# One step of gate and up columns, one block of sums: the down weights' sums spread over the steps, in tiles that they share with that step's product

## The chip, the cores and the metric

The kernel runs on one core of a Trainium2 chip. Five engines work side by side there, each in its own written order, and wait for one another through semaphores: TensorE (PE, matmuls into PSUM), VectorE (DVE, element by element), ScalarE (ACT, casts, copies and activations), GpSimd (POOL, hardly used in the part that matters here) and SyncE (SP), which issues the transfers between the chip's main memory and the on-chip tiles. The metric is device microseconds of one execution; lower is better. Before the change the median of 3 runs is 1890.63 us (1890.01 to 1895.91).

## The reference

One decoder layer over 1024 tokens of width 1024: three attention mixers, a merge and an output projection, then a gated MLP with a short convolution. The change lies in the MLP:

```python
def conv_ffn(h, w_gate, w_up, conv_w, conv_b, w_down):
    a = h @ w_gate
    a = lax.conv_general_dilated(a, conv_w[:, None, :], window_strides=(1,),
                                 padding=[(CONV_WIDTH - 1, 0)],
                                 dimension_numbers=('NWC', 'WIO', 'NWC'),
                                 feature_group_count=a.shape[-1]) + conv_b
    return (jax.nn.gelu(a) * (h @ w_up)) @ w_down
```

`h` is [1024, 1024], `w_gate` and `w_up` are [1024, 2816], `w_down` is [2816, 1024], all float32.

## The kernel before

The matrix products are made from pairs of rounded numbers: each operand is split into a high half (an ACT cast, `qhi`, L1544) and a low half (a DVE subtraction, `qlo`, L1545), and three matmuls (L1572, L1573, L1574) stand for one exact product. Large products are made by a scheme with seven block products instead of eight: operands are cut in four quarters, and sums of quarters are multiplied (`seven`). Its right operands (the activations, B11, T1 and so on) stay on chip; its left operands are the weights and sums of the weights (S1 to S4).

`gate_up` walks over the 2816 columns in 10 steps of two column blocks (f0 = 2, 4, ..., 20; the pair f0 = 0 is made earlier). A step loads two pieces of w_gate and two of w_up (`qraw`, L1556, three buffers), makes the sums (`qS`, L1563) and halves, and calls `seven` twice, once into `ga`, once into `ua`. The tiles `ua` have the names xh6 and xh7. Then DVE multiplies the activated gate `gc` by `ua` (L1641), and SP stores it to `s_act` (L1643). Inside `seven`, PE writes a partial product into a T tile of PSUM (two buffers), DVE adds u1 to it (`u2`, then after a second product on the same tile `u3`, L1589), ACT copies one quarter of the result straight to its destination (L1599), and DVE adds the other three.

The product with `w_down` (`down`) needs the sums S1 to S4 of its own weights. They are made ahead, during `gate_up`: `down_sums(k)` loads two blocks of 128 rows of w_down into the tiles xh4 and xh5 (L1654, L1655), makes four sums in place on DVE (L1660) and stores them to `s_sums` (L1661). There are 11 such blocks; the text calls them by k, 0 to 10. At the start of `down`, xh4 and xh5 take the first activation rows (L1683).

Outside of `down`'s transfers the order of the instructions on each engine is not that of the code: a scheduler places each as early as its own estimate of times lets it go, subject to the tiles. So the sums, written for the steps f0 = 8 to 18, stand earlier on DVE: one block after another, as soon as xh4 and xh5 are free again. Products of neighbouring calls of `seven` also overlap on PE.

Of the kernel before, what the change touches and what calls it, by code (L numbers as in the profile page):

```python
# [12 lines left out]
F32 = mybir.dt.float32  # L13
# [5 lines left out]
P = 128  # L19
D = 1024  # L20
T = 1024
# [146 lines left out]
class Builder:  # L168
# [1461 lines left out]
    def gate_up(self, sp):  # L1630

        nc, a = self.nc, self.a
        hs = [slice(0, 512), slice(512, 1024)]
        for f0 in range(2, NF, 2):
            ga = self.gate_tiles(sp)
            self.seven(self.left_ops(a["w_gate"], f0), [[z[:, 2 + s.start:2 + s.stop] for s in hs] for z in ga])
            gc = self.convolve(f0, ga, sp)
            ua = [self.t(self.xp, [P, T], F32, f"xh{6 + i}") for i in range(2)]
            self.seven(self.left_ops(a["w_up"], f0), [[z[:, s] for s in hs] for z in ua])
            for i in range(2):  # L1640
                nc.vector.tensor_tensor(out=gc[i], in0=gc[i], in1=ua[i], op=ALU.mult)  # L1641
                if f0 + 2 < NF:
                    nc.sync.dma_start(self.s_act[(f0 + i) * P:(f0 + i + 1) * P, :], gc[i])  # L1643
            if 8 <= f0 < 20:
                for k in range((f0 - 8) * 11 // 12, (f0 - 6) * 11 // 12):
                    self.down_sums(k)
        return gc

    def down_sums(self, k):

        nc, w = self.nc, self.a["w_down"]
        lo, hi = slice(0, 512), slice(512, 1024)
        top, bottom = (self.t(self.xp, [P, T], F32, f"xh{n}") for n in (4, 5))
        nc.sync.dma_start(top, w[k * P:(k + 1) * P, :])  # L1654
        nc.sync.dma_start(bottom, w[(k + NF // 2) * P:(k + NF // 2 + 1) * P, :])  # L1655
        for n, o, x, y, op in ((0, bottom[:, hi], top[:, hi], bottom[:, hi], ALU.add),
                               (2, top[:, hi], top[:, lo], top[:, hi], ALU.subtract),
                               (1, top[:, lo], bottom[:, hi], top[:, lo], ALU.subtract),
                               (3, bottom[:, lo], bottom[:, lo], top[:, lo], ALU.subtract)):
            nc.vector.tensor_tensor(out=o, in0=x, in1=y, op=op)  # L1660
            nc.sync.dma_start(self.s_sums[n, k], o)  # L1661
# [262 lines left out]
```

## Time and profile before

| | |
|---|---|
| median of 3 runs | 1890.63 us |
| lowest, highest | 1890.01, 1895.91 us |
| the profiled execution's own time | 1894.6 us |
| its span, first to last instruction | 1892.8 us |
| mean granted clock of TensorE | 0.996 |
| busy: PE, DVE, ACT, POOL | 98%, 71%, 49%, 21% |
| DMA, mean over the span | 121 GB/s |

The profile is of one execution, and its times count from the span's first instruction. PE writes and reads deeply pipelined, so consecutive matmuls of 0.39 us start 0.227 us apart. The steps of `gate_up` lie between about 1263 and 1685 us, the sums of the down weights (L1660) between 1298.3 and 1447 us, the first matmul of `down` (L1787) at 1668.5. A wait is booked on the engine that stands idle, with the instruction that ended it. For SP the profile shows when it issues a transfer, and the chain of waits shows for some transfers the time from issue to landing.

### The profile page before, as it was taken

The page shows a single profiled execution, that of the slowest core. Times are in us where ns is not written, and L with a number is a line of the kernel's source. Part 1 is how long each engine was busy: PE and PEld are TensorE (multiplying, and loading weights), DVE is VectorE, ACT ScalarE, POOL GpSimd, SP SyncE. Part 2 cuts the span into 40 slices and gives each one's busy share as a digit, 9 for nine tenths or more (in the row PEclk, how much of TensorE's full clock was granted, in tenths as well). Part 3 has the DMA queues.
Part 4 walks back from the last instruction along what each step waited for, and adds up shares of the span by engine and source line. Part 5 has one row for each costly group of instructions (what it writes and reads, how often), then busy time and mean ns, then how long its engine had stood idle before and what let it go on. Part 6 is the DMA issues. An engine that isn't in the chain of part 4 may idle for free.

```text
span 1892.8 us, 30670 instructions
## 1 busy us (share of the span) xinstructions
PE 1847.5 (98%) x10663; PEld 1623.0 (86%) x10663; DVE 1345.5 (71%) x2825; ACT 926.1 (49%) x1987; POOL 406.2 (21%) x586
## 2 busy tenths in 40 slices
PE   8999999999999999999989999999999999999999
PEld 8999999999988888888878888888877888878887
DVE  7664777776875766856588766679887677776865
ACT  4443566565544654555587423445333334344443
POOL 2223655565522323213132220000000000000000
PEclk9999999999999999999999999999999999999999
DMA  6345222323221132222343745525666322267433
GB/s 209 112 140 136 81 81 74 81 82 89 76 74 56 54 95 66 65 65 57 108 142 104 239 154 175 172 84 173 229 216 205 100 67 82 80 203 236 139 100 123
DMA packets 201472, 228.38 MB, mean 121 GB/s; under 512 B 43634, under 2 KB 149122, under 8 KB 201317
## 3 DMA queue, kind: packets, MB, share of 16 engines
q1 hardware_dynamic: 201252, 226.29, 38.9%
q8 instruction: 84, 1.38, 0.3%
q14 instruction: 72, 0.58, 0.1%
q0 software_dynamic: 64, 0.13, 0.0%
HBM read 162.12 MB, written 64.25 MB: 120 GB/s over the span
## 4 chain that ended last, share of the span: by engine, by line
PE 78%; DVE 10%; DMA 6%; issue 3%; ACT 2%; POOL 1%; SPq 0%; DVEq 0%; ACTq 0%; POOLq 0%
PE D L259 9%; PE D L258 9%; PE D L260 9%; PE T L797 4%; PE O L821 2%; PE S L685 2%; PE O L820 2%; PE S L259 2%; PE S L260 2%; PE S L258 2%; PE S L689 2%; PE S L1789 2%; PE S L1787 2%; PE S L1788 2%; PE S L1573 1%
## 5 line engine op out<-in xcount | busy, mean ns | idle before, releaser
L713 ACT ACTIVATE p<-S,mf 128x512 f32<-128x512 f32 (+3 forms) x320 | 174.2, 548 | 102.7 <-DVE mf L704 94.4
L805 DVE TENSOR_TENSOR pTl<-T,pTh 128x512 fp32r<-128x512 f32 (+2 forms) x248 | 151.0, 616 | 81.1 <-ACT pTh L804 79.4
L258 PE MATMUL D<-whi,xh 128*128 128x256 f32 (+2 forms) x680 | 199.8, 294 | 2.4 <-ACT whi L234 2.4
L1544 ACT CAST qhi<-qS 128x512 fp32r<-128x512 f32 x157 | 97.4, 622 | 207.4 <-PE O L1788 57.1
L259 PE MATMUL D<-wlo,xh 128*128 128x256 f32 (+2 forms) x680 | 193.3, 284 | 2.3 <-DVE wlo L235 2.3
L260 PE MATMUL D<-whi,xl 128*128 128x256 f32 (+2 forms) x680 | 192.7, 283 | 0.0
L804 ACT CAST pTh<-T 128x512 fp32r<-128x512 f32 (+2 forms) x248 | 128.1, 531 | 121.7 <-PE T L797 109.6
L259 PE MATMUL D<-xl,whi 128*128 128x512 f32 x448 | 176.5, 394 | 0.0
L762 POOL TENSOR_SCALAR p<-p,den,gates 128x384 f32<-128x384 f32 (+3 forms) x160 | 108.4, 689 | 270.8 <-DVE den L756 168.7
L258 PE MATMUL D<-xh,whi 128*128 128x512 f32 x368 | 152.2, 413 | 0.0
L1545 DVE TENSOR_TENSOR qlo<-qS,qhi 128x512 fp32r<-128x512 f32 x157 | 107.8, 691 | 54.1 <-ACT qhi L1544 53.6
L260 PE MATMUL D<-xh,wlo 128*128 128x512 f32 x368 | 145.0, 394 | 0.0
L797 PE MATMUL T<-c,p 128*128 128x128 f32 x864 | 130.1, 274 | 6.9 <-POOL p L762 4.1
L258 PEld LDWEIGHTS D<-whi,xh 128*128 128x128 f32 x680 | 129.5, 190 | 4.7 <-ACT whi L234 3.2
L259 PEld LDWEIGHTS D<-wlo,xh 128*128 128x128 f32 x680 | 129.6, 191 | 3.8 <-DVE wlo L235 2.9
L260 PEld LDWEIGHTS D<-whi,xl 128*128 128x128 f32 x680 | 129.3, 190 | 0.0
L235 DVE TENSOR_TENSOR wlo<-wraw,whi 128x512 fp32r<-128x512 f32 (+2 forms) x136 | 102.1, 761 | 31.8 <-ACT whi L234 28.7
L820 PE MATMUL O<-pTh,VV 128*128 128x256 f32 x448 | 119.4, 290 | 2.0 <-DVE osum L886 1.9
L821 PE MATMUL O<-pTl,VV 128*128 128x256 f32 x448 | 116.6, 284 | 2.2 <-DVE pTl L805 2.2
L762 POOL TENSOR_SCALAR p<-p,den 128x256 f32<-128x256 f32 (+3 forms) x160 | 89.8, 576 | 125.6 <-ACT es L753 46.5
L685 PE MATMUL S<-U,X 128*128 128x256 f32 (+2 forms) x320 | 107.8, 342 | 4.8 <-ACT p L713 4.7
L797 PEld LDWEIGHTS T<-c,p 128*128 128x128 f32 x864 | 101.1, 141 | 12.5 <-POOL p L762 7.8
(443 smaller groups left out, 5253.0 us busy)
## 6 DMA issues: line engine op xcount, KB each, us to landing
wraw<-w_in SPq DMA_DIRECT2D x96, 256.0 KB
s_gate<-stage SPq DMA_DIRECT2D x48, 256.0 KB
qraw<-w_up SPq DMA_DIRECT2D x24, 512.0 KB
qraw<-w_gate SPq DMA_DIRECT2D x22, 512.0 KB
xh<-w_down SPq DMA_DIRECT2D x22, 512.0 KB
s_sums<-xh SPq DMA_DIRECT2D x44, 256.0 KB
qS<-s_sums SPq DMA_DIRECT2D x44, 256.0 KB
s_act<-gc SPq DMA_DIRECT2D x20, 512.0 KB
```

What stands on the lines that cost most here:

```text
L258: nc.tensor.matmul(out, lh, rh, start=(k == 0), stop=False)
L259: nc.tensor.matmul(out, lh, rl, start=False, stop=False)
L260: nc.tensor.matmul(out, ll, rh, start=False, stop=(k == n - 1))
L685: nc.tensor.matmul(p, z["x"][:, z["qs"]], u[:, ks], start=True, stop=False)
L713: nc.scalar.activation(pt, z["tiles"][n][:, :w], AF.Exp, bias=z["m"], scale=-1.0, accum_out=den[:, n, q:q + 1])
L762: nc.gpsimd.tensor_scalar(pt, pt, d0[:, q:q + 1], 1.0 if gate is None else gate, op0=ALU.mult, op1=ALU.mult)
L797: nc.tensor.transpose(p[:, c0:c0 + P], z["t"][:, k:k + P], self.ident)
L804: nc.scalar.copy(ph[:, lo:hi], p[:, lo:hi])
L805: nc.vector.tensor_tensor(out=pl[:, lo:hi], in0=p[:, lo:hi], in1=ph[:, lo:hi].bitcast(F32), op=ALU.subtract)
L820: nc.tensor.matmul(ow, vv[:, kj, :], parts["h"][:, cs], start=(b_first and s == 0), stop=False)
L821: nc.tensor.matmul(ow, vv[:, kj, :], parts["l"][:, cs], start=False, stop=(b_last and s == len(bank) - 1))
L1545: nc.vector.tensor_tensor(out=lo, in0=src, in1=hi.bitcast(F32), op=ALU.subtract)
```

## The change

The sums of block k = 0 to 8 are now called in the step f0 = 2, 4, ..., 18, one each, and use the tiles xh6 and xh7, the same that hold that step's up product; blocks 9 and 10 are called in the steps f0 = 6 and 12, with xh4 and xh5 as before.

```diff
-            if 8 <= f0 < 20:
-                for k in range((f0 - 8) * 11 // 12, (f0 - 6) * 11 // 12):
-                    self.down_sums(k)
+            if f0 < 20:
+                self.down_sums(f0 // 2 - 1, (6, 7))
+            if f0 in (6, 12):
+                self.down_sums(8 + f0 // 6, (4, 5))
         return gc
 
-    def down_sums(self, k):
+    def down_sums(self, k, tags):
...
-        top, bottom = (self.t(self.xp, [P, T], F32, f"xh{n}") for n in (4, 5))
+        top, bottom = (self.t(self.xp, [P, T], F32, f"xh{n}") for n in tags)
```

From L1654 on, lines of the changed kernel have a number one higher (the sums are L1661 there, their stores L1662, the loads L1655 and L1656).

In the rows that follow, names carry running numbers: `xh4_4002` is one use of the tile xh4. DVE, at the end of the step f0 = 6, from its last product with the up tile to the addition `u3` of the next call of `seven`. Before:

```order
L1641 TENSOR_TENSOR gc_3593_16495<-gc_3593_16495,xh6_3595_16505 128x1024
L1589 TENSOR_TENSOR u2_3647_16694<-u1_3646_16693,T_3650_16697 128x512
L1563 TENSOR_TENSOR qS4_3693_16971<-qraw_3689_16963,qS2_3691_16967 128x512
L1545 TENSOR_TENSOR qlo_3695_16974<-qraw_3688_16961,qhi_3694_16973 128x512
L1545 TENSOR_TENSOR qlo_3697_16978<-qS1_3690_16965,qhi_3696_16977 128x512
L1660 TENSOR_TENSOR xh5_4003_18534<-xh4_4002_18533,xh5_4003_18534 128x512
L1660 TENSOR_TENSOR xh4_4002_18533<-xh4_4002_18533 128x512
L1545 TENSOR_TENSOR qlo_3699_16982<-qS2_3691_16967,qhi_3698_16981 128x512
L1660 TENSOR_TENSOR xh4_4002_18533<-xh5_4003_18534,xh4_4002_18533 128x512
L1660 TENSOR_TENSOR xh5_4003_18534<-xh5_4003_18534,xh4_4002_18533 128x512
L1563 TENSOR_TENSOR qS1_3721_17115<-qraw_3719_17111,qraw_3720_17113 128x512
L1589 TENSOR_TENSOR u3_3648_16695<-u1_3646_16693,T_3650_16697 128x512
```

The same place now:

```order
L1641 TENSOR_TENSOR gc_3597_16519<-gc_3597_16519,xh6_3599_16529 128x1024
L1589 TENSOR_TENSOR u2_3655_16742<-u1_3654_16741,T_3658_16745 128x512
L1545 TENSOR_TENSOR qlo_3684_16888<-qS4_3670_16861,qhi_3683_16887 128x512
L1563 TENSOR_TENSOR qS4_3701_17019<-qraw_3697_17011,qS2_3699_17015 128x512
L1661 TENSOR_TENSOR xh7_3629_16674<-xh6_3628_16673,xh7_3629_16674 128x512
L1661 TENSOR_TENSOR xh6_3628_16673<-xh6_3628_16673 128x512
L1661 TENSOR_TENSOR xh6_3628_16673<-xh7_3629_16674,xh6_3628_16673 128x512
L1661 TENSOR_TENSOR xh7_3629_16674<-xh7_3629_16674,xh6_3628_16673 128x512
L1589 TENSOR_TENSOR u3_3656_16743<-u1_3654_16741,T_3658_16745 128x512
L1545 TENSOR_TENSOR qlo_3703_17022<-qraw_3696_17009,qhi_3702_17021 128x512
```

The four sums of a block stand in a row, directly ahead of `u3`, and in such steps the first low half of the next product stands behind them. In the other kind of step (f0 = 4, 8, 12, 16) that low half stands ahead of the sums; there are five of the one kind and four of the other. The second block that this step had before is gone.

SP, in the same step, from the store of the first half of `gc` on. Before:

```order
L1643 DMA s_act_21_86<-gc_3594_16496 128x1024
L1661 DMA s_sums_22_87<-xh5_3941_18226 128x512
L1654 DMA xh4_4002_18533<-w_down 128x1024
L1556 DMA qraw_3719_17111<-w_up 128x4x256
L1655 DMA xh5_4003_18534<-w_down 128x1024
L1643 DMA s_act_21_86<-gc_3593_16495 128x1024
L1556 DMA qraw_3720_17113<-w_up 128x4x256
```

Now:

```order
L1643 DMA s_act_21_86<-gc_3598_16520 128x1024
L1656 DMA xh7_3629_16674<-w_down 128x1024
L1556 DMA qraw_3727_17159<-w_up 128x4x256
L1643 DMA s_act_21_86<-gc_3597_16519 128x1024
L1655 DMA xh6_3628_16673<-w_down 128x1024
L1662 DMA s_sums_22_87<-xh7_3629_16674 128x512
L1662 DMA s_sums_22_87<-xh6_3628_16673 128x512 x2
L1662 DMA s_sums_22_87<-xh7_3629_16674 128x512
L1556 DMA qraw_3728_17161<-w_up 128x4x256
```

The loads of the block follow the two stores of `gc`, whose product has just read the tiles, and the second load of w_up stands behind the four stores of the sums (in the other kind of step ahead of them).

ACT, around its copy into xh6 for the up product of the step f0 = 8, with the semaphores that each instruction waits for. Before:

```order
L1544 CAST qhi_3673_16835<-qraw_3658_16805 128x512 [waits DVE_49,PE_49]
L1544 CAST qhi_3675_16839<-qS4_3662_16813 128x512 [waits PE_49]
L1544 CAST qhi_3694_16973<-qraw_3688_16961 128x512 [waits DMAHW5_49,DVE_49,PE_49]
L1599 COPY xh6_3655_16801<-S_3680_16846 128x512 [waits DVE_49,PE_49]
L1544 CAST qhi_3696_16977<-qS1_3690_16965 128x512 [waits PE_49,Activation_49]
```

Now:

```order
L1544 CAST qhi_3702_17021<-qraw_3696_17009 128x512 [waits DMAHW4_49,DVE_49,PE_49]
L1544 CAST qhi_3704_17025<-qS1_3698_17013 128x512 [waits PE_49]
L1544 CAST qhi_3706_17029<-qS2_3699_17015 128x512 [waits DVE_49,PE_49]
L1599 COPY xh6_3663_16849<-S_3688_16894 128x512 [waits DMAHW4_49,DMAHW2_49,DMAHW5_49,DVE_49,PE_49]
L1544 CAST qhi_3708_17033<-qraw_3697_17011 128x512 [waits PE_49,Activation_49]
```

The copy has moved behind two more casts and waits for three DMA semaphores: xh6 has held a block of sums in between.

## Rows read from the trace of the kernel before

**Rows 1.** The page, part 1: busy time of each engine, its share of the span and its instructions.

```profile
PE 1847.5 (98%) x10663; PEld 1623.0 (86%) x10663; DVE 1345.5 (71%) x2825; ACT 926.1 (49%) x1987; POOL 406.2 (21%) x586
```

**Rows 2.** Busy time of the engines in two stretches of 180 us: the one with the sums and the one behind it. Columns: stretch, its length, busy us of each engine (and instructions), granted clock of PE, DMA share, GB/s.

```profile
1300.00:1480.00 180.00, 172.05 (x747) 140.41 (x746) 144.67 (x223) 65.18 (x98) 0.00 (x0) 0.99 0.63 213
1480.00:1660.00 180.00, 180.00 (x796) 149.05 (x795) 131.62 (x192) 71.12 (x105) 0.00 (x0) 1.00 0.27 84
```

**Rows 3.** Waits of PE from 1300 to 1480 us, all that there are: total us, times, longest. From 1480 to 1660 us there is none.

```profile
PE T L1572 <- DVE u L1589: 8.0, 5, 3.2
```

**Rows 4.** Timeline of PE, two of these five waits, and two matmuls behind the longer one. Columns: start us, us, instruction, and in brackets the idle time before it and what ended it.

```profile
1437.73 0.47 PE L1572 MATMUL T<-r,qhi 128*128 128x512 f32 x1 [0.76 <-DVE u L1589]
...
1460.17 0.47 PE L1572 MATMUL T<-r,qhi 128*128 128x512 f32 x1 [3.16 <-DVE u L1589]
...
1461.19 0.63 PE L1572 MATMUL T<-r,qhi 128*128 128x512 f32 x1
1461.62 0.63 PE L1573 MATMUL T<-r,qhi 128*128 128x512 f32 x1
```

**Rows 5.** Waits of DVE for transfers from 1300 to 1480 us: total us, times, longest.

```profile
DVE xh L1660 <- DMA xh<-w_down: 7.7, 5, 2.2
DVE xh L1660 <- DMA s_act<-gc: 6.3, 2, 3.3
DVE qS L1563 <- DMA qraw<-w_gate: 3.5, 1, 3.5
```

**Rows 6.** Timeline of DVE ahead of the two waits of rows 4.

```profile
1433.04 0.69 DVE L1660 TENSOR_TENSOR xh<-xh,xh 128x512 f32<-128x512 f32 x1 [3.02 <-DMA s_act<-gc]
...
1436.90 0.68 DVE L1589 TENSOR_TENSOR u<-u,T 128x512 f32<-128x512 f32 x1
...
1458.72 0.69 DVE L1563 TENSOR_TENSOR qS<-qraw,qraw 128x512 f32<-128x512 f32 x1 [3.54 <-DMA qraw<-w_gate]
1459.34 0.68 DVE L1589 TENSOR_TENSOR u<-u,T 128x512 f32<-128x512 f32 x1
```

**Rows 7.** Timeline of SP there: the loads of the first activation rows for the down stage, and the w_gate load that L1563 waits for.

```profile
1450.82 1.74 SPq L1683 DMA_DIRECT2D xh<-s_act  x4
1452.66 0.38 SPq L1556 DMA_DIRECT2D qraw<-w_gate  x1
```

**Rows 8.** Timeline of DVE in an undisturbed step without sums, from the last product of a step on.

```profile
1542.27 1.22 DVE L1641 TENSOR_TENSOR gc<-gc,xh 128x1024 f32<-128x1024 f32 x1
...
1551.49 0.69 DVE L1589 TENSOR_TENSOR u<-u,T 128x512 f32<-128x512 f32 x1 [5.86 <-PE T L1574]
1552.09 0.69 DVE L1545 TENSOR_TENSOR qlo<-qraw,qhi 128x512 fp32r<-128x512 f32 x1
...
1556.79 0.69 DVE L1563 TENSOR_TENSOR qS<-qraw,qraw 128x512 f32<-128x512 f32 x1 [0.97 <-DMA qraw<-w_up]
...
1561.91 0.69 DVE L1589 TENSOR_TENSOR ga<-u,D 128x512 f32<-128x512 f32 x1 [2.23 <-PE D L1574]
```

**Rows 9.** Timeline of SP in the same step.

```profile
1543.51 0.34 SPq L1643 DMA_DIRECT2D s_act<-gc  x1
1552.81 0.37 SPq L1556 DMA_DIRECT2D qraw<-w_up  x1
```

**Rows 10.** The chain of waits from 1300 to 1480 us, some of its transfers: time of issue, us until the chain goes on behind the landing, what.

```profile
1324.00 3.58 DMA xh<-w_down
...
1340.16 5.17 DMA xh<-w_down
...
1386.30 5.74 DMA s_act<-gc
...
1436.41 2.05 DMA s_sums<-xh
...
1446.21 4.54 DMA s_sums<-xh
...
1452.66 5.97 DMA qraw<-w_gate
```

**Rows 11.** Timeline of PE in the step of rows 8: the first matmul into the T tile that `u3` has freed, and the first that reads the next product's low half.

```profile
1554.91 0.39 PE L1572 MATMUL T<-r,qhi 128*128 128x512 f32 x1
...
1555.37 0.39 PE L1574 MATMUL S<-xl,qlo 128*128 128x512 f32 x1
```

**Rows 12.** Timeline of ACT in the step of rows 8: the copy into xh6, a cast, and the copy of u1 for the next product.

```profile
1551.94 0.59 ACT L1599 COPY xh<-S 128x512 f32<-128x512 f32 x1
1554.48 0.62 ACT L1544 CAST qhi<-qraw 128x512 fp32r<-128x512 f32 x1 [1.95 <-PE S L1573]
...
1558.13 0.58 ACT L1594 COPY u<-S 128x512 f32<-128x512 f32 x1
```

**Rows 13.** Timeline of SP at the end of the step f0 = 18, its last store of `gc`.

```profile
1658.21 0.32 SPq L1643 DMA_DIRECT2D s_act<-gc  x1
```

**Rows 14.** Timeline of DVE behind it: a low half for the first product of `down`, and the addition `u3`.

```profile
1661.17 0.69 DVE L1545 TENSOR_TENSOR qlo<-xh,qhi 128x512 fp32r<-128x512 f32 x1 [1.79 <-ACT qhi L1544]
...
1666.18 0.69 DVE L1589 TENSOR_TENSOR u<-u,T 128x512 f32<-128x512 f32 x1 [3.60 <-PE T L1574]
```

**Rows 15.** Timeline of PE there: the first matmuls of `down` that read the low halves of its two operands.

```profile
1668.93 0.39 PE L1788 MATMUL S<-qlo,qhi 128*128 128x512 f32 x1
...
1669.61 0.61 PE L1789 MATMUL S<-qhi,qlo 128*128 128x512 f32 x2
```

## The prediction

> **What bounds the kernel now.** I read the page first: TensorE (PE) is busy 98% of the span [rows 1]. A change that adds no work to PE and takes none from it can therefore only win or lose the moments in which PE stands still, or runs at the lower clock. So the next view is PE by stretches. The sums of the down weights (L1660) run from about 1300 to 1447 us. I compare the 180 us around them with the 180 us behind them, in which the same gate and up products run without sums: 747 matmuls against 796, at the same 180 us [rows 2]. One matmul of the undisturbed stretch takes 180 / 796 = 0.226 us, so the stretch with the sums has lost 49 x 0.226 = 11.1 us. In the stretch behind it PE waits for nothing and the mean granted clock is 1.00; the one with the sums has 0.99.
>
> The waits of PE name the cause of 8.0 of the 11.1 us: five waits of the first matmul of a T product (L1572) for an addition of VectorE (DVE), `plus(u, ...)` at L1589, which must read the old T tile before PE may write it [rows 3]. The timeline shows the shortest of the five, 0.76 us, and the longest, 3.16 us [rows 4]. After the longest one PE fell to the lower of its two clock levels: matmuls there last 0.63 us and start 0.43 us apart, where 0.39 and 0.226 are normal. The other 3.1 us are this and some slow first matmuls.
>
> Why is the addition late? DVE is not full (144.7 of 180 us [rows 2]), but it works strictly in its written order, and in this stretch it stands before L1660 for transfers: 7.7 us for loads of w_down, 6.3 us in waits put down to a store, 3.5 us for a load of w_gate [rows 5]. Two cases in its timeline: 3.02 us of idling ahead of a sum at 1433.04, with the addition for T only at 1436.90 and PE's wait ending at 1437.73; and 3.54 us ahead of L1563 at 1458.72, where the w_gate load is late, with the addition at 1459.34 and PE's longest wait ending at 1460.17 [rows 4, 6]. That load was late because SP, which issues in order too, had queued it behind the loads of xh4 and xh5 at 1450.82, and so went out at 1452.66 only [rows 7]. Before, two blocks of sums fall on a step of two columns; the order of DVE for the kernel before shows them spread between the additions.
>
> **The change, part by part.** Sums removed: none. There are still 11 blocks, each of two 512 KB loads, four DVE subtractions or additions and four stores, so no engine's total changes. What moves is when and in which tiles.
>
> (1) Blocks 9 and 10 keep xh4 and xh5 and stand at the same two places as the first two blocks before, where PE did not wait. Cost 0. The loads of xh4 and xh5 for the down stage, which before went out just ahead of the late w_gate load, follow block 10 at once; the third block's loads stood there before and cost PE nothing. Cost 0.
>
> (2) The other nine blocks go one per step into xh6 and xh7. By the order, they stand directly behind the last addition of a step: four in a row, between `qS4` and the addition `u3`. What they meet there is seen in an undisturbed step. DVE ends the step's last product (L1641) at 1543.49, does three short operations, and then idles 5.86 us until T is done at 1551.49 [rows 8]. SP can issue the load of xh6 right behind the store at 1543.51 [rows 9], so at about 1543.9. Nothing in the trace shows that load in that place. The nearest rows are the loads of w_down: 3.58 and 5.17 us from issue to landing; a store of gc takes 5.74 and the slowest weight load 5.97 [rows 10]. Lower end 3.58; upper end 5.74 + 3.58 = 9.3, if the store ahead of it and the load go one after the other. I take 5.2, the upper load row, because a store and a w_up load are in flight too. Then the block arrives at 1549.1, and four operations of 0.69 us [rows 6], which start 0.60 apart back to back (1551.49 to 1552.09 in [rows 8]), end at 1549.1 + 3 x 0.60 + 0.69 = 1551.6: 0.1 us behind the time at which the addition starts now. PE needs that addition for T at 1554.91, and the low half made at 1552.09 by 1555.37 [rows 11]. From 1551.6 both are ready at about 1552.3 and 1552.9, so some 2.5 us are left, and the load may take 5.2 + 2.5 = 7.7 us before PE waits. Cost at 5.2: 0. At 9.3: 1.6 us in each of nine steps = 14.4.
>
> The Trainium skill ("DMA: Bandwidth & Descriptors", Queues, rings and completion order) says that each DMA engine consumes its descriptors in ring order, so the load stands behind the store issued 0.4 us before it. No row here isolates such a pair; by this rule alone one would lean to the upper end, 9.3, and the sum would lose the 14.4 us.
>
> (3) A new wait on ScalarE (ACT): the copy L1599 of the next up product into xh6 must now wait until the stores of the sums have left xh6 (the order shows three DMA semaphores on it). In the undisturbed step it runs at 1551.94 [rows 12]. The third sum ends at 1549.1 + 1.2 + 0.69 = 1551.0, its store is issued at about 1551.3 and lands 2.05 to 4.54 us later [rows 10], so the copy starts at 1553.4 to 1555.8. Queued behind it on ACT are two casts of 0.62 us and the copy of u1 at 1558.13 [rows 12]; with 0.58 + 1.24 us in between they are on time even from 1555.8. Cost 0, and 0 to 1 us per step if the load comes at the upper end.
>
> (4) SP: in five of nine steps the second w_up load stands behind the four stores of sums. Now it goes out at 1552.81 [rows 9], when a low half frees its buffer; that moves by 0.1 us. DVE already waits 0.97 us for it and then idles 2.23 us before 1561.91 [rows 8]. If it takes 5.97 instead of its 3.98 us behind the stores, the 2.0 us fit into those 2.23. Cost 0; with that cover gone, whatever exceeds 2.23 moves the additions behind it.
>
> (5) The last block now stands ahead of the down stage. The store before its xh6 load is at 1658.21 [rows 13]; with 5.2 us the load lands at 1663.8, the sums end at 1666.3, the addition that ran at 1666.18 [rows 14] slips by 0.1. The two low halves for the first down product, of which one was made at 1661.17 [rows 14], now come behind it, at 1667.6 and 1668.2; PE reads them at 1668.93 and 1669.61 [rows 15]. Cost 0; at 9.3 us 2.8.
>
> Sum: 11.1 us off, 0 back. The profiled execution took 1894.6 us (span 1892.8), so 1883.5. The median of the three runs is 1890.63, 4.0 below; part of that difference may be the longest wait with its slow matmuls, which then isn't there to be won. From the median the full 11.1 would give 1879.5. I take the middle of the two, **1881.5 us**, that is 9.1 off the median.
>
> **The rivals.** First, part is given back: loads land at about 8.5 us in the five steps with the late w_up load and the low half behind the sums, 0.8 us over the limit each and 0.6 for the slow matmuls behind it (3.1 us over the five waits of before), 5 x 1.4 = 7, giving 1888.5, no change that can be told (0.3% is 5.7 us, about what a measurement of this kernel can tell). For it: DVE already waited 0.97 us for w_up without any sums [rows 8]. Against: the stretch with sums had two blocks per step and still only 8.0 us of waits [rows 3].
>
> Second, slower: the load of xh6 is exposed in every step. The pair of tiles holds one block, and its load can start only when the product has been read, where before the next block's loads went out while other work was going on. At 9.3 us the nine steps lose 14.4 and the entry of the down stage 2.8, together 17.2, giving 1881.5 + 17.2 = 1898.7; it turns slower than can be told as noise from 14.8 given back, 1.6 per step, a load of 9.3 us or more. For it: the two rows of 5.74 and 5.97 under load [rows 10]. Against: DMA moves 84 GB/s in the undisturbed stretch against 213 with the sums [rows 2], so each transfer will have fewer beside it. The Trainium skill ("Trainium Kernel Development and Optimization", Best Practices) asks for double buffers so that transfers lie beside compute, which speaks against this change; the trace of before, with a single pair xh4 and xh5, agrees with it, at 7.7 us of waits for w_down [rows 5].
>
> Third, the waits have nothing to do with the sums and stay: 1890.6. Against it stands the undisturbed stretch, which has no wait of PE at all [rows 2]. That the scheduler undoes the spreading is excluded by the order, which has one block per step.
>
> **How the numbers follow.** Forecast 0.68; part given back 0.16 and waits stay 0.03, both no change; slower 0.13. The forecast's own spread is 1879.5 to 1883.5 with some 2.5 us of run to run difference on the low side, so the range begins at 1877. Above it takes in the first and the third rival and ends at 1890; outside lie the slower one and a few per cent below. Faster by over 0.3% is 0.68, within 0.3% 0.19, slower 0.13.
>
> **What would show it.** Right: no wait of PE for L1589 between 1300 and 1660, some 795 matmuls in both stretches, clock 1.00; DVE waits of 2 to 5 us before the first sum of each step that nobody waits for; the copy L1599 waiting 1 to 4 us for stores. Wrong: PE waits at T, at the first low half of a product, or at L1788 on entering the down stage, and loads of xh6 that take over 7.7 us.

## The result and the profile after

The changed kernel takes 1881.61 us (median of 5 runs, 1879.12 to 1884.49), the kernel before 1892.33 us in the runs beside it (1890.01 to 1895.91). The ratio is 0.9938, with a 95% interval of 0.9925 to 0.9952: faster, by 9 to 14 us, or 0.5 to 0.75%. The forecast was 1881.5 us.

The two stretches of [rows 2] in the changed kernel, with the same columns:

```profile
1300.00:1480.00 180.00, 180.00 (x796) 149.05 (x795) 144.81 (x214) 70.86 (x106) 0.00 (x0) 1.00 0.46 154
1480.00:1660.00 180.00, 179.74 (x793) 148.52 (x792) 138.99 (x206) 67.54 (x102) 0.00 (x0) 1.00 0.45 152
```

PE is at 796 matmuls in the first stretch, where it had 747, and the transfers are even, 154 and 152 GB/s in place of 213 and 84. All waits of PE from 1300 to 1700 us, which answer to [rows 3]:

```profile
PE S L1788 <- ACT qhi L1544: 0.5, 1, 0.5
PE S L1790 <- DVE qlo L1545: 0.3, 1, 0.3
PE D L1572 <- DVE ga L1589: 0.3, 1, 0.3
```

The five waits for `u` are gone; all three that are left lie at the entry of the down stage, from 1656.97 us on. Two pairs of matmuls bound the gate and up stage sharply: the first of L1572 and the first of the down stage. In the timeline of PE before the change:

```profile
1239.61 0.39 PE L1572 MATMUL T<-xl,qhi 128*128 128x512 f32 x1
...
1668.70 0.39 PE L1787 MATMUL S<-qhi,qhi 128*128 128x512 f32 x1
```

and after it:

```profile
1237.86 0.39 PE L1572 MATMUL T<-xl,qhi 128*128 128x512 f32 x1
...
1655.87 0.39 PE L1788 MATMUL S<-qhi,qhi 128*128 128x512 f32 x1
```

That is 429.1 us before and 418.0 after, 11.1 less, the 11.1 us counted in [rows 2]. The profiled spans differ by 13.0 us (1892.8 and 1879.8); 1.75 us of that lie ahead of the stage, where nothing was changed, and the down stage, from the start of its first matmul to the end of the last, takes 219.8 and 219.7 us. So this stage length tells kernels apart more finely than the whole time, whose start moves by some us from run to run, and the experiments below give both. One run each of e1, e5 and e11 took 2.7 to 7.6 ms, and the ratios leave it out.

One step of the changed kernel, which answers to [rows 8, 9, 11, 12]. DVE:

```profile
1567.52 1.22 DVE L1641 TENSOR_TENSOR gc<-gc,xh 128x1024 f32<-128x1024 f32 x1
...
1574.66 0.69 DVE L1661 TENSOR_TENSOR xh<-xh,xh 128x512 f32<-128x512 f32 x1 [3.78 <-DMA xh<-w_down]
...
1576.11 1.42 DVE L1661 TENSOR_TENSOR xh<-xh,xh 128x512 f32<-128x512 f32 x2
1577.44 0.68 DVE L1589 TENSOR_TENSOR u<-u,T 128x512 f32<-128x512 f32 x1
```

SP, with the load of xh6, the four stores of the sums and the second load of w_up:

```profile
1568.76 0.33 SPq L1643 DMA_DIRECT2D s_act<-gc  x1
1569.14 0.42 SPq L1655 DMA_DIRECT2D xh<-w_down  x1
1575.38 2.50 SPq L1662 DMA_DIRECT2D s_sums<-xh  x4
1578.75 0.38 SPq L1556 DMA_DIRECT2D qraw<-w_up  x1
```

ACT's copy into xh6:

```profile
1579.00 0.59 ACT L1599 COPY xh<-S 128x512 f32<-128x512 f32 x1 [1.87 <-DMA s_sums<-xh]
```

and PE's next T product:

```profile
1580.16 0.39 PE L1572 MATMUL T<-r,qhi 128*128 128x512 f32 x1
```

The load is issued 0.40 us behind the end of L1641 (1568.74); the first sum starts 5.52 us later. DVE idles 3.78 us there, and nobody waits for it: u3 ends at 1578.12, T is overwritten at 1580.16, 11.4 us behind the product.

What SP stands for has changed most. Its waits from 1300 to 1480 us before the change:

```profile
SPq L1661 <- DMA xh<-w_down: 36.3, 10, 4.9
...
SPq L1654 <- DMA s_sums<-xh: 12.5, 9, 2.9
SPq L1556 <- DVE qlo L1545: 11.0, 13, 2.1
SPq L1655 <- DMA s_sums<-xh: 5.1, 7, 1.8
SPq L1683 <- DMA s_sums<-xh: 3.0, 1, 3.0
```

and after it:

```profile
SPq L1556 <- DVE qlo L1545: 90.6, 18, 10.2
...
SPq L1662 <- DMA xh<-w_down: 5.2, 1, 5.2
SPq L1655 <- DMA s_sums<-xh: 1.4, 1, 1.4
SPq L1684 <- DMA s_sums<-xh: 0.8, 2, 0.5
```

Before, SP stood 20.6 us (12.5 + 5.1 + 3.0) until stores of sums had left the one pair of tiles. Now that is 2.2 us, and SP stands 90.6 us ready at the weight loads (L1556), until their buffers are free. The weight loads themselves gained little by that: before, too, SP stood ready at 13 of the 18 in this stretch until DVE's low half had freed the buffer. What changed more for them is how long they took, which is told behind e13.

### The profile page after: what moved, and what is told of

The parts are those of the page before. It is cut to its first block, busy times and chain, and to the rows that moved or that the text cites. A ratio compares the mean times of both kernels' runs of the same rounds, so it can differ in the third digit from the quotient of the medians.

```text
span 1879.8 us, 30674 instructions
## 1 busy us (share of the span) xinstructions
PE 1842.3 (98%) x10663; PEld 1619.8 (86%) x10663; DVE 1349.6 (72%) x2825; ACT 926.3 (49%) x1987; POOL 406.7 (22%) x586
## 4 chain that ended last, share of the span: by engine, by line
PE 90%; DVE 5%; DMA 2%; ACT 2%; issue 1%; POOL 1%; SPq 0%; DVEq 0%; ACTq 0%; POOLq 0%
PE D L259 9%; PE D L258 9%; PE D L260 9%; PE T L797 5%; PE S L1574 3%; PE S L1572 3%; PE S L1573 3%; PE O L821 3%; PE O L820 2%; PE S L685 2%; PE T L1574 2%; PE T L1573 2%; PE T L1572 2%; PE D L1572 2%; PE D L1574 2%; PE D L1573 2%
```

## The experiments

All times in us; the kernel before took 1892.05 to 1892.82 in these sets. "Stage" runs from the first matmul of L1572 to the first of the down stage, "down" from there to the end of the last matmul, both in the profiled run; each PE wait named is from the profile.

| run | median | ratio to before, 95% | stage | down |
|---|---|---|---|---|
| before | 1892.33 | | 429.1 | 219.8 |
| changed | 1881.61 | 0.9925 to 0.9952 | 418.0 | 219.7 |
| e1_spread_old_tiles | 1892.54 | 0.9985 to 1.0012 | 426.0 | 220.0 |
| e2_shared_dense | 1894.93 | 1.0000 to 1.0021 | 418.2 | 230.8 |
| e3_one_block | 1881.46 | 0.9922 to 0.9953 | 418.0 | 219.8 |
| e4_load_later | 1884.47 | 0.9931 to 0.9969 | 418.0 | 224.7 |
| e5_spread_own_tiles | 1884.12 | 0.9930 to 0.9969 | 418.0 | 220.6 |
| e6_before_no_adds | 1890.27 | 0.9986 to 1.0006 | 426.5 | 219.8 |
| e7_before_no_early_rows | 1888.81 | 0.9976 to 0.9995 | 424.9 | 219.8 |
| e9_shared_dense_early | 1883.88 | 0.9941 to 0.9971 | 419.5 | 219.8 |
| e10_load_much_later | 1881.63 | 0.9927 to 0.9956 | 418.0 | 220.1 |
| e11_before_pool_queue | 1887.67 | 0.9963 to 0.9988 | 424.1 | 219.8 |
| e12_before_pool_adds | 1910.72 | 1.0076 to 1.0120 | 447.0 | 220.6 |
| e13_before_pool_both | 1900.30 | 1.0022 to 1.0061 | 429.7 | 219.8 |

### Is there anything left to win? (e3)

```diff
-            if f0 < 20:
-                self.down_sums(f0 // 2 - 1, (6, 7))
-            if f0 in (6, 12):
-                self.down_sums(8 + f0 // 6, (4, 5))
+            if f0 == 6:
+                self.down_sums(0, (4, 5))
...
-                src = self.s_sums[int(name[1]) - 1, k]
+                src = self.s_sums[int(name[1]) - 1, 0]
```

> The changed kernel without the sums of ten of the eleven blocks: their loads, additions and stores are left out, one block is made at f0 = 6 in xh4 and xh5, and the down stage reads that block in place of all. Theory (the sums are hidden to the last in the changed kernel): within 2 us of the changed kernel's 1881.6 us, 796 matmuls in every 180 us of the gate and up stage in both. Rival (the sums still cost something there, as loads beside the weight loads or as DVE time): 1870 to 1878 us.

1881.46 us and a stage of 418.0: the same as with all eleven blocks. The sums are hidden to the last in the changed kernel; the rival falls.

### What makes the gain: the calls, the tiles, or the number per step? (e1, e5, e2, e9)

Calls one per step, all in the old pair of tiles:

```diff
-                self.down_sums(f0 // 2 - 1, (6, 7))
+                self.down_sums(f0 // 2 - 1, (4, 5))
```

> The calls of the changed kernel, one block per step from f0 = 2 on, but all in xh4 and xh5; DVE's order puts the sums where the kernel before has them, one block behind another, up to 1447 us. Theory (the tile that is shared with the up product is what holds the blocks apart; the step in which a block is called does nothing): 1890 to 1895 us, five PE waits for the addition L1589 again, some 429 us from the first matmul of L1572 to the first of the down stage. Rival (the calls do it): 1880 to 1884 us, 418 us.

1892.54 us, as before the change: the calls alone do nothing, as the scheduler takes each block as soon as the tiles are free. PE waits five times again, 6.3 us in all, though one of the five, 0.5 us, is for a cast and not for `u`. The stage, in the same order as before the change, took 426.0 us here and 429.1 there: the loss in that order differs by some us between executions.

One block per step in the old pair, held back by a copy of one element of the up tile:

```diff
+            if f0 == 2:
+                self.down_sums(9, (4, 5))
+                self.down_sums(10, (4, 5))
+            if f0 < 18:
+                self.down_sums(f0 // 2 - 1, (4, 5), ua)
...
+        for z in (top, bottom) if tie else ():
+            nc.vector.tensor_copy(z[:, 0:1], tie[1][:, 0:1])
```

> One block per step, but in xh4 and xh5: blocks 9 and 10 first, then blocks 0 to 7 one per step, held back by a copy of one element of the up tile into each of xh4 and xh5 ahead of the loads; only block 8 stays in xh6 and xh7. Theory (spreading is what gains, and the shared tile is only the means of it): within 2 us of the changed kernel's 1881.6 us, no PE wait for the addition L1589 from 1263 to 1650 us, and no wait of ACT's copy L1599 for stores of sums, which were 3.9 us at the most and cost nothing. Rival A (sharing has a price on ACT that the shared version pays): 1 to 4 us per step in eight steps come back, 1850 to 1875 us. Rival B (xh6 and xh7 themselves are needed, for instance as they leave xh4 and xh5 to the act rows): as slow as before the change, 1890 us and more.

The stage is 418.0 us: holding the blocks back is what gains, and the shared tile is one means of it. Three runs took 1882.65, 1882.72 and 1885.53 us; in the profiled one, the longest, the down stage has 0.9 us more than in the changed kernel (220.6), and the rest is not told apart from the spread of the runs. ACT's copy no longer waits for stores, and nothing comes of it: rival A falls, and so does B.

The shared pair, with the calls of before (two blocks in each of the five last steps):

```diff
-            if f0 < 20:
-                self.down_sums(f0 // 2 - 1, (6, 7))
-            if f0 in (6, 12):
-                self.down_sums(8 + f0 // 6, (4, 5))
+            if 8 <= f0 < 20:
+                for k in range((f0 - 8) * 11 // 12, (f0 - 6) * 11 // 12):
+                    self.down_sums(k, (6, 7))
```

> The sums stay in xh6 and xh7, but are called as before the change: none in the steps f0 = 2, 4, 6, then one block at f0 = 8 and two in each of the five steps f0 = 10 to 18. Theory (what counts is that a step has one block, which fits between the product with ua and the next copy into xh6): the second block of a step loads only when the stores of the first have left the tiles, about 5.2 us of load, 1.9 us of sums and up to 4.5 us of store after the first load was issued, then takes 5.2 us of load, 1.9 of sums and 2 to 4.5 of store again, so that the copy into xh6 comes some 9 to 12 us late in each of five steps. Of that 4 us are covered; PE loses 5 to 8 us in each, so the run takes 1905 to 1925 us. Rival (the tiles are what counts, whatever the number of blocks per step, since transfers and sums lie in DVE's idle time): no PE waits, 1880 to 1885 us, like the changed kernel.

Both theories missed. The stage took 418.2 us, so two blocks per step cost it nothing: DVE's order puts the second block behind a `u3`, and the copy into xh6 moves behind it. But the down stage took 230.8, 11.1 more, since the last block stood at its entry. PE there:

```profile
1672.47 0.49 PE L1789 MATMUL S<-qhi,qlo 128*128 128x512 f32 x1 [3.18 <-DVE qlo L1545]
...
1677.97 0.80 PE L1787 MATMUL S<-qhi,qhi 128*128 128x512 f32 x1 [4.77 <-ACT xh L1599]
1678.57 0.63 PE L1788 MATMUL S<-qlo,qhi 128*128 128x512 f32 x1
1678.99 0.63 PE L1789 MATMUL S<-qhi,qlo 128*128 128x512 f32 x1
```

Two waits of 8.0 us, the longer one behind ACT's copy into xh6, which stood until stores of the sums had left; then PE runs at the lower of its two levels, matmuls 0.42 us apart. So the same dense calls, but early, with none at the entry:

```diff
+            for k in range(f0 - 2, min(f0, 11)):
+                self.down_sums(k, (6, 7))
```

> All eleven blocks in xh6 and xh7, two per step in f0 = 2 to 10 and the last in f0 = 12. In the run with two per step in f0 = 10 to 18 the gate and up stage lost nothing (418.2 us against 418.0) and all of the loss, 11 us, lay at the entry of the down stage. Theory now (what counts is that a block's place follows the product, where DVE's order puts the additions for PE ahead of late sums, and that none lies at the entry of the down stage; one per step is not needed): stage 418 us, down stage 219 to 220 us, 1880 to 1884 us. Rival (two per step cost something as they do in the kernel before): 2 us or more of PE waits in the five steps, 1886 us and more.

1883.88 us, stage 419.5, down stage 219.8. The loss at the entry is gone. Two per step cost 1.5 us of stage against one per step, with two waits of PE of 0.6 us in all, so one per step is the better, but by little; most of the gain comes from where a block stands.

### How late may the load come? (e4, e10)

```diff
-        nc.sync.dma_start(top, w[k * P:(k + 1) * P, :])
+        if tags[0] == 6:
+            nc.gpsimd.memset(top[:, 0:1024], 0.0)
+        (nc.gpsimd if tags[0] == 6 else nc.sync).dma_start(top, w[k * P:(k + 1) * P, :])
```

> The changed kernel with the load into the first of the two tiles, xh6, later in each of nine steps: it goes through POOL's queue, behind a memset of that tile on POOL, and the order of DVE stays as it was. Theory (the load may take 7.7 us from the end of the product before PE waits, 2.5 us more than the 5.2 us taken): the first sum starts 6.3 to 8 us behind the end of L1641 instead of 5.1 to 6.0; while it starts within 7.7 us PE waits for nothing and the time is 1880 to 1884 us; for each us beyond 7.7 PE waits one us more, plus 0.6 us of slow matmuls, in each of nine steps. Rival (there is no such margin, what the load is late PE is late): 1 to 2.5 us lost in each of nine steps, 1890 to 1904 us.

In eight steps the first sum started 5.6 to 6.7 us behind the product, up to 1 us later than in the changed kernel, and the stage stayed at 418.0. In the last step it came at 8.6 us in place of 6.2: its load, from 1646.97 to 1654.17, took 7.2 us, beside the first loads of the down stage. DVE and PE there:

```profile
1654.17 0.69 DVE L1663 TENSOR_TENSOR xh<-xh,xh 128x512 f32<-128x512 f32 x1 [7.15 <-DMA xh<-w_down]
...
1657.55 0.69 DVE L1545 TENSOR_TENSOR qlo<-xh,qhi 128x512 fp32r<-128x512 f32 x1
```

```profile
1658.29 0.49 PE L1791 MATMUL S<-qlo,qhi 128*128 128x512 f32 x1 [1.33 <-DVE qlo L1545]
...
1660.39 0.50 PE L1790 MATMUL S<-qhi,qhi 128*128 128x512 f32 x1 [0.99 <-ACT xh L1599]
```

PE waits for the low half behind the sums, and the down stage took 224.7 us, 5.0 more. This is the one place at which the margin ran out: 2.4 us of lateness cost 5.0.

```diff
+        if tags[0] == 6 and k < 8:
+            nc.gpsimd.memset(top[:, 0:8], 1.0)
+            for _ in range(6):
+                nc.gpsimd.tensor_tensor(out=top[:, 0:8], in0=top[:, 0:8], in1=top[:, 0:8], op=ALU.mult)
+            for c in range(0, T, T // 2):
+                nc.gpsimd.dma_start(top[:, c:c + T // 2], w[k * P:(k + 1) * P, c:c + T // 2])
```

> The changed kernel with the load of xh6 issued later in eight of nine steps: POOL makes a memset and six small multiplications on the tile and then issues the load in two halves; block 8 stays as it was, and the orders of PE, DVE and ACT are those of the changed kernel. In the changed kernel the first sum starts 5.5 to 6.4 us behind the end of L1641, the addition u3 8.3 to 9.2, and PE's next T product 11.4 us behind it in four of these steps and 13.2 in the other four. Theory (margin of 2.3 us, then one us of PE for each us): with first sums at x us, the four steps of 11.4 us lose x minus 8.1 each, and slow matmuls where that is over 1 us; the other four lose nothing up to x = 9.9. For x = 9 that is 3.6 us, 1884 to 1888 us; for x up to 8.1 nothing. Rival (the later sums delay all that follows on DVE and ACT, the copy into xh6 and the casts behind it among them, so PE loses in all eight steps and before x = 8.1): 1889 to 1900 us.

1881.63 us, stage 418.0. The second half of the tile was not held back by the multiplications, so the first sum, which reads that half, came as early as ever (4.8 to 6.3 us); only the last two sums came later. The four ended 8.9 to 10.8 us behind the product, against 8.3 to 9.3 in the changed kernel, and the latest, 1.5 us beyond that range, fell into steps in which PE's T product starts at 13.2. Nothing was lost, as the theory has it for these, but the edge at 11.4 was not reached, and what a us beyond it costs inside the stage stays open.

### What delayed the additions in the kernel before? (e7, e6, e11, e12, e13)

Without the early loads of activation rows:

```diff
         for k in range(lead):
-            rows(k, lo)
-            rows(k, hi)
+            nc.gpsimd.memset(act[k], 0.0)
```

> The kernel before, without the four loads of the first two activation rows into xh4 and xh5 (L1683); POOL fills the tiles with zeros instead. Theory (SP, in order, stood at these loads until the last stores of the sums had left, with the load of w_gate behind them): the load of w_gate goes out up to 5 us earlier, the longest PE wait of 3.2 us and the slow matmuls behind it are gone, the four others, 4.8 us, stay: 1886 to 1889 us, some 424 us of stage instead of 429. Rival (the load was late for its buffer or for the traffic): the wait stays, 1890 to 1895 us.

1888.81 us, 3.2 less than before; the wait of 3.2 us and its slow matmuls are gone, and 0.5 us for a cast is left in that place. The load of w_gate went out at 1451.70 in place of 1452.66: 1 us earlier, not 5. DVE's low half that frees the buffer for it, before:

```profile
1451.49 0.69 DVE L1545 TENSOR_TENSOR qlo<-qraw,qhi 128x512 fp32r<-128x512 f32 x1
```

and the same low half, the sum that reads the load, and SP in e7:

```profile
1450.99 0.68 DVE L1545 TENSOR_TENSOR qlo<-qraw,qhi 128x512 fp32r<-128x512 f32 x1
...
1455.82 0.69 DVE L1563 TENSOR_TENSOR qS<-qraw,qraw 128x512 f32<-128x512 f32 x1 [1.14 <-issue]
```

```profile
1451.70 0.38 SPq L1556 DMA_DIRECT2D qraw<-w_gate  x1
```

Before, the buffer was free at 1452.18, so SP's queue held the load up by 0.5 us and not more. The sum now starts 2.9 us earlier (1455.82 against 1458.72 [rows 6]): 0.5 us by SP's queue, 0.5 by the earlier low half, and 1.9 because the load, without the four others beside it, took 4.04 us by its landing in the trace, where it had taken 5.97 [rows 10]. So most of this wait came from the company of the transfers and not from SP's order.

Without the additions, raw halves stored:

```diff
-            nc.vector.tensor_tensor(out=o, in0=x, in1=y, op=op)
             nc.sync.dma_start(self.s_sums[n, k], o)
```

> The kernel before, with all loads of w_down and all stores to s_sums, but without the 44 additions and subtractions between them (raw halves are stored). Theory (PE waits since DVE, in its order, stands for the loads and has the additions for T behind it; the traffic alone is harmless): the waits of DVE for w_down are gone and of the five PE waits at most the one for the late w_gate load, 3.2 us and 1.6 of slow matmuls, stays: 1881 to 1887 us. Rival (213 GB/s of traffic is what delays the loads of the weights): PE waits 5 us or more in this stretch, 1889 us or more.

The theory fell: 1890.27 us, no change that can be told, with a stage of 426.5. Its order has the stores right behind the loads, so that the chain of load, store and next load in the one pair of tiles keeps SP and the transfers busy, and what DVE now stands for are the weights. DVE's waits for transfers from 1300 to 1480 us:

```profile
DVE qS L1563 <- DMA qraw<-w_gate: 17.4, 3, 9.5
DVE qS L1563 <- DMA qraw<-w_up: 13.7, 4, 6.5
```

The 9.5 us wait comes from this, in the timeline of SP:

```profile
1369.39 0.46 SPq L1556 DMA_DIRECT2D qraw<-w_gate  x1
1370.07 0.48 SPq L1654 DMA_DIRECT2D xh<-w_down  x1
1371.74 0.33 SPq L1655 DMA_DIRECT2D xh<-w_down  x1
1376.28 2.08 SPq L1660 DMA_DIRECT2D s_sums<-xh  x4
1379.10 0.33 SPq L1654 DMA_DIRECT2D xh<-w_down  x1
1379.53 0.41 SPq L1556 DMA_DIRECT2D qraw<-w_gate  x1
```

The second load of w_gate stood behind a whole round of load, four stores and next load, and PE waited 5.2 us for what hung on it. So SP's queue became a theory of its own, against DVE's order and against traffic. The chain on POOL's queue:

```diff
-        nc.sync.dma_start(top, w[k * P:(k + 1) * P, :])
-        nc.sync.dma_start(bottom, w[(k + NF // 2) * P:(k + NF // 2 + 1) * P, :])
+        nc.gpsimd.dma_start(top, w[k * P:(k + 1) * P, :])
+        nc.gpsimd.dma_start(bottom, w[(k + NF // 2) * P:(k + NF // 2 + 1) * P, :])
...
-            nc.sync.dma_start(self.s_sums[n, k], o)
+            nc.gpsimd.dma_start(self.s_sums[n, k], o)
```

> The kernel before, with the loads of w_down and the stores of the sums issued by POOL in place of SP; tiles, additions on DVE and traffic stay. Leaving out the additions had not taken the PE waits away: there SP stood in the chain of load, store and next load, with weight loads queued behind, and DVE waited 31 us for those. Theory SP (the kernel before loses time since SP, in order, stands at this chain and issues weight loads late): the PE waits go, stage 418 to 420 us, 1880 to 1884 us. Theory DVE (DVE stands at the sums with the additions for T behind): waits of DVE at L1660 for w_down stay at 7 us or more, PE waits stay at 4 us or more, only the late w_gate load is mended, 1885 to 1890 us. Theory traffic: nothing changes, 1890 us and more.

1887.67 us, stage 424.1: some 5 of the 11 us, or 1.9 against the 426.0 of e1. DVE still stood 14.0 us for loads of w_down and 7.9 for loads of w_up, and PE waited 3.0 us once for `u`, directly behind a sum, and 0.4 for a low half. So SP's queue is not the whole cause, and as the traffic stayed at 206 GB/s, its amount is not either. More does not follow: the scheduler gave PE, DVE and ACT another order here, as it did in e6, e12 and e13 (in e1 and e7 they have the order of before), so none of these four runs takes away one thing alone. The additions on POOL (e12), and then both edits together (e13):

```diff
-            nc.vector.tensor_tensor(out=o, in0=x, in1=y, op=op)
+            nc.gpsimd.tensor_tensor(out=o, in0=x, in1=y, op=op)
```

> The kernel before, with the additions of the sums on POOL in place of DVE; tiles, loads and stores on SP stay. Theory SP: SP still stands in the chain, longer still as an addition on POOL takes longer; weight loads are late, DVE waits for them at L1563, and PE waits 4 us or more: 1886 to 1893 us. Theory DVE: without sums in its order DVE is on time, PE waits under 1 us: 1880 to 1884 us. Theory traffic: 1890 us and more.

> The kernel before, with both on POOL: its queue issues the loads of w_down and the stores of the sums, and it makes the additions; only the traffic is left of the old arrangement for SP and DVE. If SP and DVE together are the whole cause: no PE wait, stage 418 us, 1880 to 1884 us. Theory traffic: weight loads still land late, waits of DVE at L1563 over 5 us, 1886 us and more.

1910.72 us, above every range but that of the traffic theory, which has no upper end, and 1900.30 with both moved. With the sums off DVE, weights were late as the SP theory has it in the first of the two (DVE waits 13.9 us for w_up and 9.9 for w_gate). In the second DVE waited less for them (3.1 and 1.6 us); but there it came to them later, as it was nearly full, and the loads still took 4.7 us in the mean, so this says little about traffic. Both runs are spoilt as a test by something else. The stretch from 1300 to 1480 us of the second:

```profile
1300.00:1480.00 180.00, 174.07 (x750) 141.31 (x751) 164.45 (x186) 66.37 (x101) 90.21 (x104) 0.99 0.62 207
```

DVE is busy 164.45 us with 186 instructions, where it was 144.67 with 223 [rows 2]: its instructions are slower, and it is nearly full. So whether SP and DVE together are the whole cause was not shown.

The traces hold one more thing that bears on it: when each transfer landed (the last update of its semaphore). In the kernel before, a weight load of 512 KB took 3.74 to 3.89 us from 1480 to 1660 us, without sums, 3.82 in the mean of 16; from 1300 to 1480 us, with them, 3.66 to 6.50, 5.07 in the mean of 18. In the changed kernel the means are 4.06 and 3.96 us; in e11, with SP ready at the loads, 4.96. Two more of the five old waits hang on such a load, as the longest does. DVE and SP ahead of the first of them:

```profile
1374.89 0.69 DVE L1563 TENSOR_TENSOR qS<-qraw,qraw 128x512 f32<-128x512 f32 x1 [1.21 <-issue]
1375.51 0.68 DVE L1589 TENSOR_TENSOR u<-u,T 128x512 f32<-128x512 f32 x1
```

```profile
1369.25 0.38 SPq L1556 DMA_DIRECT2D qraw<-w_gate  x1
```

This load went out 0.03 us behind the low half that freed its buffer, so SP did not hold it up. It took 5.56 us, DVE idled 1.21 us for it with `u3` behind, and PE's wait of 1.43 us ended at 1376.33. The wait of 1.56 us that ended at 1417.61 is of the same kind (a load of 4.93 us). With the longest, these three make 6.1 of the 8.0 us; the other two, 1.04 and 0.76 us, stand behind sums at L1660 whose own loads were late. An estimate from these times: with loads of 3.82 us the three waits would be some 4 us shorter in all. So a slower weight load beside the transfers of a block is a third part of the cause, which no run takes away alone, and how the 11.1 us divide among the three stays open.

## Why the prediction was right, point by point

**The sum.** 11.1 us off, 0 back: the stage shows 11.1 off, the down stage 0.1. That forecast and median agree to 0.1 us is luck: 9.1 us were taken off a median of 1890.63, and 10.7 came off one of 1892.33. Halving the last 4 us was a hedge on the median shown, 1890.63; in later sets the kernel before took 1892.05 to 1892.82, and 1892.33 - 11.1 is 1881.2. The reason given for the hedge has some ground: in e1, the same order, the longest waits were shorter and the stage lost 8 us in place of 11.

**The load of xh6**, taken as 5.2 us within 3.58 and 9.3: 5.07 to 6.03 us from issue to the first sum in nine steps. The sums ended 8.3 to 9.3 us behind the product (8.1 forecast), and PE wanted T at 11.4, as read from the undisturbed step. The upper end, the load behind the whole store, was wrong: with a store 0.4 us ahead the load took at most 2.5 us longer than the quickest load of w_down in [rows 10], 3.58, and not 5.74. On POOL's queue (e4), away from SP's stores, it took 4.2 to 5.3 us in eight steps, 0.5 us less in the mean. The rule of the Trainium skill ("DMA: Bandwidth & Descriptors", Queues, rings and completion order) on ring order is not contradicted by that, but the price that was hung on it is.

**ACT's copy** was to start at 9.9 to 12.3 us behind the product and to wait 1 to 4 us: it started at 9.9 to 12.3 and waited 1.6 to 3.9, at no cost; e5, without the wait, gained nothing.

**SP and w_up**: DVE's waits for w_up, 0.9 us at the longest in the first stretch and 1.0 in the second, are as in the undisturbed step (0.97 in [rows 8]).

**The last block** at the entry: its load took 5.75 us, and the entry lost nothing. But its price when late was set too low: 2.8 us at a load of 9.3, where e4 lost 5.0 at a sum 2.4 us late. Of the slower rival's two places the entry was the narrow one (e4, e2); in the nine steps no run reached the edge.

**The causes of the old waits** were the step that fell short. DVE standing at L1660 in its order was read as the cause of four waits, and SP's queue as that of the fifth, the longest. The traces leave two waits, 1.8 us, to L1660. The other three hang on a w_gate load that took 4.9 to 6.0 us in place of 3.8, and SP's queue made 0.5 us of the longest one's lateness (e7). A weight load that is slow beside the transfers of the sums was not among the causes that the prediction weighed. e6, which takes the additions away and gains nothing, and e11, which frees SP and gains some us, fit more than one cause, but both have another order of instructions. The sum did not need the division, since holding the blocks back takes all of them away. The prediction also counts two blocks to a step before. The trace has three: their first sums start at 1345.8, 1358.9 and 1373.0 us, between the ends of the products at 1344.7 and 1386.3. So the change goes from three to one, and the two per step of e9 are not the case of before.

**The rivals.** Part given back: no; e3 shows nothing left. Waits stay: no. Double buffers, which the Trainium skill ("Trainium Kernel Development and Optimization", Best Practices) asks for, were not tried; with a single pair the stage is already at the 418.0 us that it takes with ten blocks left out, so another pair has nothing to win there.

## What to carry to other kernels

Side work that an in-order queue takes as soon as its buffer is free can do harm although every engine has room: tie it to the point at which the engine that carries it has idle time, by a shared tile or a small copy, see that no weight load is queued behind its chain (e6), and look at how long the loads beside its transfers take, not only at when they go out. Then look at the seams: the last piece of such work beside the start of the next stage had the smallest margin here. To judge it, measure a stage between two instructions of the bounding engine, and leave the side work out once: that gives the floor.

## What the runs showed of the hardware

DVE's instructions with two operands in SBUF, the on-chip memory beside PSUM, get slower while POOL adds. Groups of DVE from 1300 to 1480 us in the kernel before (instruction, count, busy us, mean ns, idle time before):

```profile
L1545 DVE TENSOR_TENSOR qlo<-qS,qhi 128x512 fp32r<-128x512 f32 x37 | 25.4, 691 | 0.1
...
L1589 DVE TENSOR_TENSOR u<-u,T 128x512 f32<-128x512 f32 x18 | 12.3, 686 | 11.3 <-PE T L1574 11.3
L1641 DVE TENSOR_TENSOR gc<-gc,xh 128x1024 f32<-128x1024 f32 x8 | 9.8, 1223 | 0.0
```

and with the additions of the sums and their transfers on POOL (e13):

```profile
L1545 DVE TENSOR_TENSOR qlo<-qS,qhi 128x512 fp32r<-128x512 f32 x38 | 40.4, 1070 | 0.5 <-ACT qhi L1544 0.5
...
L1641 DVE TENSOR_TENSOR gc<-gc,xh 128x1024 f32<-128x1024 f32 x8 | 14.5, 1816 | 0.0
L1589 DVE TENSOR_TENSOR u<-u,T 128x512 f32<-128x512 f32 x18 | 12.2, 678 | 5.4 <-PE T L1574 5.3
```

The low halves went from 691 to 1070 ns and the product with `ua` from 1223 to 1816, while additions with one operand in PSUM stayed at 0.68 us. POOL's own additions took 1314 to 1349 ns there, about twice DVE's. The Trainium skill ("SBUF — State Buffer", Terms) says that DVE and GpSimd share one pair of ports, and that whoever comes second is blocked for the other's whole instruction; the trace agrees: 43 of the 66 low halves of that stretch still took 0.7 us, and the other 23 up to 2.3. Moving 42 additions from DVE to POOL raised DVE's busy time by 20 us in place of taking 29 off (42 x 0.69).

The other surprise is what company costs a transfer of 512 KB. Weight loads took 3.82 us in the mean without the sums and 5.07 with them; the load of xh6 took 5.07 to 6.03 us to its first sum behind a store, and 7.2 in e4 beside the burst of loads at the start of the down stage.
